# Two heads of a chunked mixer: where row broadcasts, staging transfers and transposing loads stand in their queues

## The chip, the cores and the metric

The kernel runs on one NeuronCore of one Trainium2 chip. The engines that matter here are TensorE (PE in the profile; its weight loads are PEld), VectorE (DVE), ScalarE (ACT), GpSimd (POOL) and SyncE (SP). SP issues the plain loads, POOL issues the transfers of this document's second part, and ACT issues the transposing loads. Each engine works through one queue in order: what stands behind a waiting instruction waits too. The metric is the device time of one launch in microseconds, lower is better. The median of three runs before is 1336.8 us, with 1336.1 us and 1338.56 us at the ends.

## What is computed

A two-layer backbone over 256 context tokens and 256 latent tokens of width 1024. Layer 0 mixes tokens with a bidirectional mLSTM of four heads, layer 1 with multi-head latent attention; a gated ConvFFN follows each. Only the mLSTM of layer 0 is touched. Cut to what matters, in each of its two directions:

```python
q, k = jnp.split(x_c @ w_qk, 2, axis=-1)               # 4 heads of 256
v = x_m @ w_v                                           # 4 heads of 512
dmat = where(tril, b[..., :, None] - b[..., None, :] + ic[..., None, :], -inf)
wmat = exp(dmat - mj[..., None]) * einsum("bhjd,bhsd->bhjs", q, k)
h = einsum("bhjs,bhse->bhje", wmat, v) / maximum(abs(sum(wmat, -1)), exp(-mj))[..., None]
out = head_rms_norm(sigmoid(h_in @ w_og) * (h_forward + h_backward)) @ w_out
```

The reference runs it in chunks of 64 with a carried state. The kernel computes the same sums over all 512 tokens at once: one 512-wide row of scores for each of four tiles of 128 tokens, weighted by exponentials of gate sums, in both directions.

## The kernel before

All matrix products are made of float32 numbers cut into a high and a low part (`split`, L460: an ACT cast makes the high part, a DVE subtraction the low one). Each product is three matmuls (`mm3`, L444): high by high, high by low, low by high. So each weight tile of 512 KB is loaded by SP, cast on ACT (L361) and subtracted on DVE (L384) before PE can use it; three such tiles `w` exist at a time.

**The loop over heads** (`build`, L2442 to L2458) interleaves two heads. While PE makes the queries and keys of head h (`w_qk`, L1024: four tiles j of 128 columns, two for the queries and two for the keys, each in two sections of 24 matmuls, so eight sections in all), DVE and ACT work on head h - 1 in small steps. After every section `tick(2, ...)` takes two steps of that background work, so a head has 16 steps. Behind the eight sections come the product of head h - 1's weights with its values (`av`, L1232) and the scores of head h (`s_mm`, L1042).

**What a background step is.** For head h - 1 the generator `head` (L1066) broadcasts two rows of gate sums over 128 partitions (tiles aB0 and aB1, DMAs on POOL's queue, L1070), adds a mask to them (Am0, Am1, DVE, L1075), makes the weights W of the four token tiles in three groups (ACT exponentials L1112, DVE products and normalisation L1113 to L1130), and transposes them on PE into PT (L1147). It ends with `t4_step(2)`, which issues two transfers from the packed weights into the DRAM tiles `t4d` (L1781). In these heads they are plain copies of 512 KB or 256 KB, the first terms of sums that later steps of the same list accumulate. Each is pinned behind the POOL instruction that was traced just ahead of it.

For head h - 2 the generator `post` (L1249) normalises the head's output and, in its second step, rearranges each of the four token tiles into two 16-bit planes (ACT, L466) and stores them in DRAM (tile hd, POOL's queue, L1265). Later, `turn_load` (L1298) reads them back transposed, one quarter at a time (tile hx, a transposing DMA on ACT's queue, L1306), and `turn_split` (L1309) cuts each quarter into the high and low parts hn (L1314 and L1315), which the output product `mout` reads after the loop.

**`mixed`** (L1285) has the order of both generators written out as 16 words, one for each step: h is a step of `head`, p one of `post`, L a `turn_load`, S a `turn_split`, a dot nothing. It runs in the stages of w_qk(2), with head 1 and the post step of head 0, and of w_qk(3), with head 2 and the post step of head 1. These two stages are what the change touches. Ahead of section 6 (tile j = 3, first half) `w_qk` calls `v_load` (L1197), which loads four value tiles vr and four gate tiles oh over POOL's queue and cuts the values.

**What sets the order.** The program is traced in this order and then ordered by a scheduler: each engine's queue takes instructions by their place in the trace, but one whose inputs and tile slot are at hand may go earlier. `behind` (L453) adds an order without a wait between two instructions of one engine. The tiles aB, Am, W, S, pl, hx, vr, oh and some others share one pool of 15 slots (tag `s2`).

Of the kernel before, what the change touches and what calls it, by code (L numbers as in the profile page):

```python
# [10 lines left out]
U16 = mybir.dt.uint16  # L11
# [405 lines left out]
class K:  # L417
# [40 lines left out]
                    mybir.DependencyClass.NoSync, mybir.DependencyReason.DATA), reason="behind")  # L458

    def split(self, hi, lo, src):  # L460
        self.nc.scalar.copy(hi, src)
        self.nc.vector.tensor_sub(lo, src, hi)

    def planes(self, dst, src):

        i = self.nc.scalar.copy(dst, src.bitcast(U16).rearrange("p (n h) -> p h n", h=2))  # L466
        return i
# [556 lines left out]
    def w_qk(self, h, nt, early=None):  # L1024
        self.qk = getattr(self, "qk", {})
        for j in range(4):
            m = (h * 2 + j) if j < 2 else (8 + h * 2 + j - 2)
            ps = self.ps("qk")
            for c in range(2):
                if early is not None and (j, c) == VE[h]:  # L1030
                    early()
                w = self.st.use(("qk", m, c))
                for kk in range(8):
                    k = 8 * c + kk
                    cs = slice(kk * 128, (kk + 1) * 128)
                    self.mm3(ps, (w[0][:, cs], w[1][:, cs]), (self.xc[k][:, 0], self.xc[k][:, 1]), k == 0, k == 15)
                self.tick(nt, ADA_Q)
            u = self.u("qk")
            self.split(u[:, 0], u[:, 1], ps)
            self.qk[h, j] = u  # L1040

    def s_mm(self, h):  # L1042
# [23 lines left out]
    def head(self, h, S, big=False):  # L1066
        nc, last = self.nc, big
# [2 lines left out]
            nc.gpsimd.dma_start(aB[d], self.ad[d, h:h + 1, :].to_broadcast([128, 512]))  # L1070
        if h == 0:
            self.t4_step(2)
        Am = [self.s2("Am0"), self.s2("Am1")]
        for d in range(2):
            nc.vector.tensor_tensor(Am[d].rearrange("p (t s) -> p t s", t=4),  # L1075
# [5 lines left out]
        for g in range(3):  # L1081
# [9 lines left out]
            for i, t in enumerate(jbs):  # L1091
                base = 256 * i if g == 0 else 0
                for d in range(2):
# [3 lines left out]
                    if d == 0:  # L1097
                        if t > 0:
                            spans.append((0, t * 128, aB[d]))
                        lo, hi = 0, (t + 1) * 128  # L1100
                    else:
# [6 lines left out]
                        lo, hi = {0: (0, 256), 1: (128, 256), 2: (0, 512), 3: (0, 512)}[t]  # L1108
# [11 lines left out]
            e = self.gcol[:, 1, jbs[0]:jbs[-1] + 1, h::32]  # L1120
# [3 lines left out]
            for i, t in enumerate(jbs):  # L1124
                big = {0: 1, 1: 0, 2: 1, 3: 0}[t]
# [15 lines left out]
        for grp in ([(t, s) for s in range(2) for t in (0, 1)], [(t, s) for s in range(2) for t in (2, 3)],  # L1141
# [3 lines left out]
            for n, (t, s) in sorted(enumerate(grp), key=lambda x: -x[1][0] * (x[1][0] > 1)):  # L1145
                src, b0 = P[t]
                q = nc.tensor.transpose(pt[:, n * 128:(n + 1) * 128], src[:, b0 + s * 128:b0 + (s + 1) * 128], self.ident)  # L1147
# [4 lines left out]
            u = self.u("PT")  # L1152
            self.split(u[:, 0], u[:, 1], pt)
            for n, x in enumerate(grp):
                self.PT[x] = u, slice(n * 128, (n + 1) * 128)
        if not last:
            self.t4_step(2)
        yield

    def head_turn(self, P):  # L1160
# [36 lines left out]
    def v_load(self, h):  # L1197
        nc = self.nc
        self.vh, self.oh = [], []
        for s in range(4):  # L1200
            r = self.s2("vr")
            nc.gpsimd.dma_start(r, self.vd[h, s])
            u = self.u("v")
            self.split(u[:, 0], u[:, 1], r)
            self.vh.append(u)
        for s in range(4):
            o = self.s2("oh")
            nc.gpsimd.dma_start(o, self.od[h, s])
            self.oh.append(o)

    def v_steps(self, h):

        nc = self.nc
        self.vh, self.oh = [], []
        for s in range(4):
            if s % 2 == 0:
                r = self.uf("vr")
            c = slice((s % 2) * 512, (s % 2 + 1) * 512)
            nc.gpsimd.dma_start(r[:, c], self.vd[h, s])
            u = self.u("v")  # L1220
            self.split(u[:, 0], u[:, 1], r[:, c])
            self.vh.append(u)
            yield
        for s in range(4):
            if s % 2 == 0:
                o = self.uf("oh")
            c = slice((s % 2) * 512, (s % 2 + 1) * 512)
            nc.gpsimd.dma_start(o[:, c], self.od[h, s])
            self.oh.append(o[:, c])
            yield  # L1230
# [53 lines left out]

    def mixed(self, head, post):  # L1285

        plan = "p hp h hL h hL . L S hLS h S S . . ."
        for step in plan.split():
            for op in step:
                if op in "hp":  # L1290
                    next(head if op == "h" else post, None)
                elif op == "L":
                    self.turn_load()
                elif op == "S":
                    self.turn_split()
            yield

    def turn_load(self):  # L1298

        h, d, e = self.turned[0]  # L1300
        if e == 3:
            self.turned.pop(0)
        else:
            self.turned[0] = h, d, e + 1
        x = self.s2("hx")
        self.nc.scalar.dma_start_transpose(x.bitcast(U16), d.rearrange("t h n -> (t h) n")[:, e * 128:(e + 1) * 128])  # L1306
        self.hx.append((h * 4 + e, x))

    def turn_split(self):  # L1309
# [134 lines left out]
    def aout_fin(self, o1, pl, xr, gate, fi, h1u, att):  # L1444
# [86 lines left out]
        def cols(t, pts, n):  # L1531
            mod(t, 0, pts)
            for k in range(0, n, 2):
                mod(t, k + 1, pts)
                split(t, k, 0)
                split(t, k + 1, 0)
                if k + 2 < n:
                    mod(t, k + 2, pts)
                split(t, k, 1)
                split(t, k + 1, 1)  # L1540
# [1063 lines left out]
```

## Time and profile before

| what | time |
|---|---|
| runs: median, lowest, highest | 1336.8, 1336.1, 1338.56 us |
| the profiled execution | 1337.46 us |
| its span, first to last instruction | 1335.3 us |
| outside the span | 2.16 us |
| DVE busy, share of the span | 1074.8 us, 80% |
| ACT busy, share of the span | 731.1 us, 55% |
| POOL busy, share of the span | 165.2 us, 12% |

The last four come from the page's first part. A group of instructions is named by its line in the kernel, its engine and its operation, with the tile written, an arrow and the tiles read. In the timeline the columns are start, duration (over all of a merged row), engine, line, operation, tiles, form and count, and in brackets the time that the engine sat idle before, with what ended it. An engine name with a q is the sequencer of that engine, which issues DMAs. In the view of one tile the last line gives the time from issue to landing of its DMAs. A matmul of 128x512 is shown with 0.39 us but the next starts about 0.23 us after it, since they are pipelined; starts, not durations, tell PE's pace.

### The profile page before, as it was taken

The page shows a single profiled execution, that of the slowest core. Times are in us where ns is not written, and L with a number is a line of the kernel's source. Part 1 is how long each engine was busy: PE and PEld are TensorE (multiplying, and loading weights), DVE is VectorE, ACT ScalarE, POOL GpSimd, SP SyncE. Part 2 cuts the span into 40 slices and gives each one's busy share as a digit, 9 for nine tenths or more (in the row PEclk, how much of TensorE's full clock was granted, in tenths as well). Part 3 has the DMA queues.
Part 4 walks back from the last instruction along what each step waited for, and adds up shares of the span by engine and source line. Part 5 has one row for each costly group of instructions (what it writes and reads, how often), then busy time and mean ns, then how long its engine had stood idle before and what let it go on. Part 6 is the DMA issues. An engine that isn't in the chain of part 4 may idle for free.

```text
span 1335.3 us, 18738 instructions
## 1 busy us (share of the span) xinstructions
PE 1324.6 (99%) x6561; PEld 1110.5 (83%) x6561; DVE 1074.8 (80%) x1784; ACT 731.1 (55%) x1275; POOL 165.2 (12%) x268
## 2 busy tenths in 40 slices
PE   9999999999999999999999999999999999999997
PEld 5877888888888888888898888888888988988886
DVE  4798957678687796987879977758899889899996
ACT  4765544446734655574644333333467768577771
POOL 0222000011101111120002011112000022120010
PEclk9999999999999999999999999999999999999999
DMA  9988948789678687885628989967876597499690
GB/s 368 332 279 281 337 164 257 233 271 306 242 239 240 179 244 199 298 277 209 223 80 272 324 263 283 278 170 187 310 245 212 179 243 205 154 317 298 228 333 36
DMA packets 122030, 327.10 MB, mean 245 GB/s; under 512 B 24792, under 2 KB 45528, under 8 KB 121664
## 3 DMA queue, kind: packets, MB, share of 16 engines
q1 hardware_dynamic: 64432, 223.50, 49.0%
q0 software_dynamic: 33360, 81.43, 22.6%
q10 hardware_dynamic: 24144, 20.98, 5.3%
q8 instruction: 51, 0.84, 0.2%
q14 instruction: 43, 0.35, 0.1%
HBM read 289.51 MB, written 57.58 MB: 260 GB/s over the span
## 4 chain that ended last, share of the span: by engine, by line
PE 87%; issue 10%; DVE 1%; DMA 1%; POOL 1%; ACT 0%; ACTq 0%; DVEq 0%; POOLq 0%
PE fin L1612 8%; PE y L450 6%; PE y L447 6%; PE y L451 6%; PE tok L447 6%; PE tok L450 6%; PE tok L451 6%; PE fin L450 6%; PE fin L451 6%; PE fin L447 6%; PE up L743 2%; PE up L447 2%; PE up L450 1%; PE up L451 1%; PE y L1455 1%
## 5 line engine op out<-in xcount | busy, mean ns | idle before, releaser
L384 DVE TENSOR_TENSOR w<-raw,w 128x1024 fp32r<-128x1024 f32 (+2 forms) x280 | 335.1, 1200 | 113.7 <-ACT w L361 109.6
L361 ACT CAST w<-raw 128x1024 fp32r<-128x1024 f32 (+2 forms) x280 | 289.7, 1036 | 248.9 <-PE tok L451 74.4
L566 DVE SCALAR_TENSOR_TENSOR junk<-ar,bc 128x1024 f32<-128x1024 f32 x128 | 155.7, 1217 | 6.0 <-DMA raw<-in_ws 2.3
L450 PE MATMUL fin<-h,w 128*128 128x512 f32 (+1 forms) x370 | 139.6, 377 | 0.0
L447 PE MATMUL fin<-h,w 128*128 128x512 f32 (+1 forms) x370 | 139.5, 377 | 0.0
L451 PE MATMUL fin<-h,w 128*128 128x512 f32 (+1 forms) x370 | 139.3, 377 | 0.0
L1612 PE MATMUL fin<-h,w 128*128 128x512 f32 (+1 forms) x636 | 113.0, 337 | 0.0
L1612 PEld LDWEIGHTS fin<-h,w 128*128 128x128 f32 x636 | 98.4, 189 | 13.4
L451 PE MATMUL qk<-xc,w 128*128 128x512 f32 x256 | 99.7, 390 | 0.3 <-DVE w L384 0.3
L447 PE MATMUL qk<-xc,w 128*128 128x512 f32 x256 | 99.9, 390 | 0.0
L450 PE MATMUL qk<-xc,w 128*128 128x512 f32 x256 | 99.6, 389 | 0.0
L450 PEld LDWEIGHTS fin<-h,w 128*128 128x128 f32 x370 | 69.6, 188 | 13.0
L447 PEld LDWEIGHTS fin<-h,w 128*128 128x128 f32 x370 | 69.6, 188 | 12.8
L451 PEld LDWEIGHTS fin<-h,w 128*128 128x128 f32 x370 | 69.6, 188 | 12.6
L384 DVE TENSOR_TENSOR wu<-raw,wu 128x1024 fp32r<-128x1024 f32 (+1 forms) x52 | 61.9, 1205 | 3.1 <-ACT wu L361 2.8
L451 PEld LDWEIGHTS qk<-xc,w 128*128 128x128 f32 x256 | 48.0, 188 | 10.6 <-DVE w L384 0.7
L450 PEld LDWEIGHTS qk<-xc,w 128*128 128x128 f32 x256 | 48.1, 188 | 10.0
L447 PEld LDWEIGHTS qk<-xc,w 128*128 128x128 f32 x256 | 48.1, 188 | 9.9
L361 ACT CAST wu<-raw 128x1024 fp32r<-128x1024 f32 (+1 forms) x52 | 52.8, 1045 | 5.5 <-DMA raw<-in_ws 5.5
L760 ACT ACTIVATE fg<-fg 128x512 f32<-128x512 f32 (+1 forms) x44 | 23.1, 525 | 57.8 <-DVE fg L758 51.7
L447 PE MATMUL tok<-w,hT 128*128 128x512 f32 x128 | 49.9, 390 | 0.0
L450 PE MATMUL tok<-w,hT 128*128 128x512 f32 x128 | 49.8, 389 | 0.0
(523 smaller groups left out, 3154.6 us busy)
## 6 DMA issues: line engine op xcount, KB each, us to landing
raw<-in_ws SPq DMA_DIRECT2D x279, 512.0 KB, 5.4
ar<-in_adaT SPq DMA_DIRECT2D x80, 512.0 KB, 5.7
t4d<-in_ws POOLq DMA_DIRECT2D x20, 512.0 KB, 8.7
zd<-in_ws POOLq DMA_DIRECT2D x18, 512.0 KB, 8.8
adaw<-in_ada SPq DMA_DIRECT2D x16, 512.0 KB, 7.9
raw<-zd SPq DMA_DIRECT2D x12, 512.0 KB, 5.7
zr<-fd ACTq DMA_DIRECT2D x33, 128.0 KB, 5.4
xmd<-xr POOLq DMA_DIRECT2D x16, 256.0 KB, 4.7
```

Source lines behind the costliest of these rows:

```text
L361: self.cast = k.nc.scalar.copy(h[:, :cols], src)
L384: i = self.k.nc.vector.tensor_sub(l[:, :n], src, h[:, :n])
L447: q = mm(out, w[0], x[0], start=start, stop=False, skip_group_check=on)
L450: mm(out, w[0], x[1], start=False, stop=False, skip_group_check=on)
L451: mm(out, w[1], x[0], start=False, stop=stop, skip_group_check=on)
L566: nc.vector.scalar_tensor_tensor(o, w, 1.0, self.bc[j], op0=ALU.mult, op1=ALU.mult, accum_out=col[:, k, j:j + 1])
L743: nc.tensor.matmul(ps[m], wk[i][:, c], hT[k][:, j], start=made[m] == 0, stop=made[m] == 23)
L760: nc.scalar.activation(tmp[:, :n], tmp[:, :n], AF.Silu)
L1455: q = mm(ps, x[a][:, ts], w[b][:, cs], start=k == 0 and n == 0, stop=k == 7 and n == 2)
L1612: self.nc.tensor.matmul(ps[:, 0:256] if x else ps, w[x][:, k * 128:(k + 1) * 128], h[:, 0:256] if x else h, start=i == 0 and not k0, stop= ...
```

## The change

Five edits in the stages of w_qk(2) and w_qk(3):

- `head` gets one more step of its own for heads 1 and 2: the broadcasts of aB alone, then a yield, then the masks. The plan's first word becomes `hp` instead of `p`, so the broadcasts are traced ahead of the plane stores instead of behind them. The masks stay in the second step and the three groups of W in the third to fifth.
- The step that makes PT moves from the tenth word to the ninth. Both come after the same section of matmuls.
- The two `t4d` transfers are no longer traced at the end of `head` but at the end of `v_load`, behind the four vr and four oh loads (for heads 1 and 2; head 0 keeps its own).
- The four turning loads move from steps 4, 6, 8 and 10 to steps 13 and 14, and each is ordered on ACT's queue behind `qcast`, the cast of the latest finished tile of w_qk. At steps 13 and 14 that is tile j = 2.
- The four turning splits move from steps 9, 10, 12 and 13 to steps 15 and 16.

```diff
     def split(self, hi, lo, src):
-        self.nc.scalar.copy(hi, src)
+        i = self.nc.scalar.copy(hi, src)
         self.nc.vector.tensor_sub(lo, src, hi)
+        return i
@@ w_qk
             u = self.u("qk")
-            self.split(u[:, 0], u[:, 1], ps)
+            self.qcast = self.split(u[:, 0], u[:, 1], ps)
@@ head
         if h == 0:
             self.t4_step(2)
+        elif not big:
+            yield
...
-        if not last:
-            self.t4_step(2)
         yield
@@ v_load
             nc.gpsimd.dma_start(o, self.od[h, s])
             self.oh.append(o)
+        if h:
+            self.t4_step(2)
@@ mixed
-        plan = "p hp h hL h hL . L S hLS h S S . . ."
+        plan = "hp hp h h h h . . h h . . LL LL SS SS"
@@ turn_load
         x = self.s2("hx")
-        self.nc.scalar.dma_start_transpose(x.bitcast(U16), d.rearrange("t h n -> (t h) n")[:, e * 128:(e + 1) * 128])
+        q = self.nc.scalar.dma_start_transpose(x.bitcast(U16), d.rearrange("t h n -> (t h) n")[:, e * 128:(e + 1) * 128])
+        self.behind(q, [self.qcast])
         self.hx.append((h * 4 + e, x))
```

No arithmetic changes, and no instruction is added or taken away on any engine.

## The prediction

> **What bounds the kernel now.** The page first.
>
> ```profile
> span 1335.3 us, 18738 instructions
> PE 1324.6 (99%) x6561; PEld 1110.5 (83%) x6561; DVE 1074.8 (80%) x1784; ACT 731.1 (55%) x1275; POOL 165.2 (12%) x268
> PE 87%; issue 10%; DVE 1%; DMA 1%; POOL 1%; ACT 0%; ACTq 0%; DVEq 0%; POOLq 0%
> ```
>
> PE is busy for 99% of the span and carries the chain that ended last. A change that takes no matmul away can win only where PE stands still. The waits of PE name four such places in the whole kernel; two lie in w_qk:
>
> ```profile
> PE PT L1147 <- DVE W L1130: 0.5, 1, 0.5
> PE qk L451 <- DVE w L384: 0.3, 1, 0.3
> ```
>
> Where are they? The timeline of PE, at the first matmul of w_qk(2), of av(1), of w_qk(3) and of av(2):
>
> ```profile
> 456.12 0.39 PE L447 MATMUL qk<-xc,w 128*128 128x512 f32 x1
> 500.98 0.39 PE L447 MATMUL av<-v,PT 128*128 128x512 f32 x1
> 513.32 0.39 PE L447 MATMUL qk<-xc,w 128*128 128x512 f32 x1
> 559.39 0.39 PE L447 MATMUL av<-v,PT 128*128 128x512 f32 x1
> ```
>
> Both stages run the same 204 instructions on PE: 192 matmuls and 12 transposes. w_qk(2) takes 500.98 - 456.12 = 44.86 us, w_qk(3) takes 559.39 - 513.32 = 46.07 us. w_qk(2) is full; w_qk(3) loses 1.21 us. The timeline of PE shows where:
>
> ```profile
> 535.31 0.39 PE L450 MATMUL qk<-xc,w 128*128 128x512 f32 x1
> 535.96 0.50 PE L451 MATMUL qk<-xc,w 128*128 128x512 f32 x1 [0.26 <-DVE w L384]
> ...
> 541.08 0.60 PE L1147 MATMUL PT<-ident,W 128*128 128x128 f32 x4
> 542.13 1.07 PE L1147 MATMUL PT<-ident,W 128*128 128x128 f32 x8 [0.46 <-DVE W L1130]
> ```
>
> First, section 4 (of 0 to 7) waits for the low part of its weights: 0.65 us between two starts instead of 0.23. Then eight of the twelve transposes wait for the last weights of head 2. With the slower starts just behind each wait these make up the 1.21 us. DVE was late both times, so what made DVE late?
>
> ```profile
> 517.76 0.55 POOL L1265 DMA_DIRECT2D hd<-pl  x1 [31.20 <-ACT pl L466]
> ...
> 519.25 0.54 POOL L1070 DMA_DIRECT2D aB<-ad  x1
> 521.53 0.54 POOL L1070 DMA_DIRECT2D aB<-ad  x1 [0.38 <-issue]
> 522.06 1.04 POOL L1781 DMA_DIRECT2D t4d<-in_ws  x2
> ...
> 523.34 0.69 DVE L1075 TENSOR_TENSOR Am<-aB,mask 128x512 f32<-128x512 f32 x1 [5.85 <-DMA aB<-ad]
> 528.25 0.69 DVE L1075 TENSOR_TENSOR Am<-aB,mask 128x512 f32<-128x512 f32 x1 [1.94 <-DMA aB<-ad]
> 528.98 0.40 ACT L1112 ACTIVATE W<-Am,gcol 128x128 f32<-128x128 f32 x1 [4.51 <-DVE Am L1075]
> 529.15 1.18 ACTq L1306 DMA_TRANSPOSE hx<-hd  x1
> 532.61 1.05 ACT L361 CAST w<-raw 128x1024 fp32r<-128x1024 f32 x1
> 534.68 1.22 DVE L384 TENSOR_TENSOR w<-raw,w 128x1024 fp32r<-128x1024 f32 x1
> ```
>
> Those rows are from the timelines of POOL, DVE and ACT, engine by engine but in order of time. The second broadcast leaves at 521.53, behind the plane stores, and its mask runs at 528.25 after idle time. ACT stands idle 4.51 us for that mask, then runs the exponentials of W back to back; the cast of section 4's weights is queued behind them, and DVE subtracts at 534.68, ready only at 535.90. PE wanted it near 535.5. The chain is: late broadcast, late mask, blocked ACT, late weights.
>
> **The change, part by part.**
>
> *Broadcasts ahead of the stores.* Nothing is added; the two issues change places with four stores. POOL was idle 31.20 us before 517.76, so both broadcasts can be out by 517.76 + 0.54 = 518.3: 3.2 us earlier for the second, or more if slots are free earlier. The view of the tile aB gives the landings, of the one issued at 519.25 and of the one issued at 521.53:
>
> ```profile
> DMA to landing us min/median/max: 4.1/4.1/4.1
> DMA to landing us min/median/max: 6.6/6.6/6.6
> ```
>
> The second mask so comes between 518.3 + 4.1 = 522.4 and 518.3 + 6.6 = 524.9, against 528.25: 3.3 to 5.8 us earlier. I take the 4.1 us, since that broadcast had the fewer stores ahead. Section 4's weights were late by about 0.4 us and the transposes' W by about 0.6 us; even 3.3 us covers both. Worth 1.21 us in w_qk(3) and nothing in w_qk(2), which has no loss. The stores leave two issues, 1.1 us, later; their readers move by some 20 us, so that costs nothing. The mask stays in the step where it was, so the extra yield costs nothing; if the order made it later after all, the 3.3 to 5.8 us are the cover.
>
> *The t4d copies behind the head's loads.* Two issues of 0.52 us each. They go behind the last gate load, ahead of the output product, whose first matmul is the second row:
>
> ```profile
> 544.68 0.54 POOL L1208 DMA_DIRECT2D oh<-od  x1 [5.80 <-DVE hn L1315]
> 571.73 0.39 PE L447 MATMUL y<-w,hn 128*128 128x512 f32 x1
> ```
>
> The copies themselves land, by the view of the tile t4d in that stage, in
>
> ```profile
> DMA to landing us min/median/max: 7.4/7.4/7.5
> ```
>  They leave the stretch of the second broadcast and enter 539 to 553, beside the loads of the output product's weights, whose first matmul is at 571.73. The price lies between 0 and, if those loads came late by the whole 7.4 us, still 0, for there are 18 us in hand. On the gain side the copies can explain at most 6.6 - 4.1 = 2.5 us of the second broadcast's landing, and part one already takes it. I count 0. Behind them on POOL stand head 3's broadcasts, 0.5 us each copy later, needed only after 571.73.
>
> [...] The second broadcast landed in 6.6 us though its copies were issued after it. [...]
>
> *Turning loads behind the third tile.* Issue times on ACT's sequencer and landing, from the view of tile hx over both stages; then, from the timelines, the subtractions of the values in both stages and the cast of the third tile in the second:
>
> ```profile
> L1306 ACTq DMA_TRANSPOSE hx<-hd x8: 1174/1237/1439, 470.4 to 533.2; - x8
> DMA to landing us min/median/max: 3.7/3.9/4.3
> ...
> 495.39 2.48 DVE L462 TENSOR_TENSOR v<-vr,v 128x512 fp32r<-128x512 f32 x4
> 548.71 0.59 ACT L461 CAST qk<-qk 128x512 fp32r<-128x512 f32 x1 [1.29 <-PE qk L451]
> 554.04 2.49 DVE L462 TENSOR_TENSOR v<-vr,v 128x512 fp32r<-128x512 f32 x4
> ```
>
> Four issues hold the sequencer 4 x 1.237 = 4.9 us. They leave 529 to 534, where ACT runs back to back anyway (gain 0 to 4.9 us on ACT, taken as 0: the exponentials ran on between the issues), and come behind the cast at 548.71. Behind them then may stand the four value casts, a weight cast, and the cast of tile j = 3. I take the cost as 0, because the value casts are traced ahead of the loads; the other end is the first rival. The splits come last: loads out by 554, landed 4 us later, splits done near 562, while hn is read from 571.73 on. The eight splits of the two stages keep their total on both engines. Head 3's broadcasts wait for the slots of these splits already (POOL idle for them at 544.68 too) and gain the slots that hx held early.
>
> *Sum.* Against the profiled execution: 1337.46 us, of which 2.16 us lie outside the span; 1335.3 - 1.2 = 1334.1 us span, 1336.3 us in all. That execution is 0.66 us above the median of 1336.8 us; against the median the forecast is 1336.8 - 1.2 = **1335.6 us**.
>
> **The rivals.**
>
> *The turning loads stand ahead of the value casts* (slower). Then the casts start 4.9 us later. Slack before: the values of head 1 are done at 495.39 + 2.48 = 497.87, 3.1 us ahead of av(1) at 500.98; of head 2 at 556.53, 2.9 us ahead of av(2). PE would wait 1.8 and 2.0 us, and the cast of tile j = 3 behind them may add some. 1336.8 - 1.2 + 3.8 = 1339.4 us. It decides once three of the four loads (3.7 us) precede the casts. For it: ACT takes its queue in order and the loads need nothing but the tile cast. Against: the values are traced first, and their loads left long before that cast, by the timeline of POOL:
>
> ```profile
> 534.22 2.20 POOL L1202 DMA_DIRECT2D vr<-vd  x4 [11.12 <-issue]
> ```
>
> *The waits stay* (no change). The broadcasts move, but DVE is as full as before: by the windows view (window, its length, then busy PE, PEld, DVE, ACT and POOL) 9.87 us of 540 to 550 and all of 550 to 560. If the order places other work, say the ada products, into the time won, weights and W come as late as now: 1336.8 us. Against: DVE idled 5.85 and 1.94 us for the broadcasts, so there is time to fill.
>
> ```profile
> 540.00:550.00 10.00, 9.54 (x49) 7.89 (x48) 9.87 (x17) 5.09 (x10) 0.54 (x1) 1.00 0.94 346
> 550.00:560.00 10.00, 10.00 (x46) 8.29 (x45) 10.00 (x15) 4.41 (x7) 1.08 (x2) 1.00 0.68 226
> ```
>
> *Half.* One wait goes, the transposes still wait, since W's last product is ordered behind DVE work of others: 1336.8 - 0.6 = 1336.2 us.
>
> **How the numbers follow.** A measurement of this kernel tells about 0.2%, 2.7 us, from no change. Forecast 56%, no change 20%, half 14%, loads ahead of the casts 10%. No case gives 2.7 us of gain: the two stages lose 1.21 us in all. I leave 3% for a better order elsewhere. Of the slower rival, which ends at 2.6 us with an open end, I put 7% over the bound. So faster 0.03, same 0.90, slower 0.07. The range takes the forecast with the scatter of the runs (0.7 us below the median to 1.8 us above), no change and half: 1334.3 to 1338.2 us.
>
> **What would show it.** Right: both aB issues ahead of hd on POOL; the second mask before 525; no idle ACT ahead of the first exponentials; no PE wait in w_qk(3), which then takes 44.9 us; loads of hx after 548; copies after the last oh. Wrong: a PE wait at the first matmul of av or of the scores; the value casts behind DMA_TRANSPOSE on ACT; a new PE wait in the output product for weights. The forecast falls if the stage after w_qk(3) starts to wait by more than 1.2 us.

## The result and the profile after

The changed kernel takes 1352.04 us (median of 5 runs, 1344.72 to 1354.74) beside 1337.19 us of the kernel before (1336.1 to 1338.56). The ratio is 1.0102, with a 95% interval of 1.0083 to 1.0121. The forecast was 1335.6 us with a range up to 1338.2: wrong in sign and outside the range.

The profiled execution is the quickest of the five, 1344.72 us, so it shows the loss at its smallest. From its page, the lines that answer to those of before (span, busy time of each engine, and the chain that ended last):

```profile
span 1342.9 us, 18743 instructions
PE 1328.1 (99%) x6561; PEld 1112.3 (83%) x6561; DVE 1074.3 (80%) x1784; ACT 731.3 (54%) x1275; POOL 165.1 (12%) x268
PE 55%; DVE 3%; issue 1%; ACTq 1%; ACT 1%; DMA 0%; DVEq 0%
```

Each engine counts as many instructions as before (the five more of the first line belong to the sequencers, which these counts leave out). But the chain, which held PE for 87% of the span, now follows PE for 55% only and passes through ACTq, the sequencer that issues the turning loads. (Its shares no longer add up to a whole, so they are not read further.) The waits of PE name what is new:

```profile
PE sc L447 <- ACT qk L461: 2.2, 2, 1.9
PE PT L1150 <- DVE W L1133: 1.7, 2, 0.9
```

The score matmuls now wait for the cast of the last tile of w_qk, j = 3, and the transposes into PT for W. Where the time goes is read from the first matmuls on PE's timeline: of w_qk(2), av(1), w_qk(3), av(2) and the output product y.

```profile
457.23 0.39 PE L447 MATMUL qk<-xc,w 128*128 128x512 f32 x1
...
502.10 0.39 PE L447 MATMUL av<-v,PT 128*128 128x512 f32 x1
...
515.58 0.39 PE L447 MATMUL qk<-xc,w 128*128 128x512 f32 x1
...
561.52 0.39 PE L447 MATMUL av<-v,PT 128*128 128x512 f32 x1
...
578.45 0.39 PE L447 MATMUL y<-w,hn 128*128 128x512 f32 x1
```

Against the starts of before (456.12, 500.98, 513.32, 559.39, 571.73) the stages compare like this. "av and scores" is from the first matmul of av to the first of the next stage.

| stage | before | after | lost |
|---|---|---|---|
| w_qk(2) | 44.86 | 44.87 | 0.01 |
| av(1) and scores | 12.34 | 13.48 | 1.14 |
| w_qk(3) | 46.07 | 45.94 | -0.13 |
| av(2) and scores | 12.34 | 16.93 | 4.59 |

The span is 7.6 us longer. Of these, 5.6 us lie in the four rows, 1.1 us ahead of w_qk(2) (457.23 against 456.12, a figure that moves by as much between kernels that do the same work there), and the rest in the output product behind. Nothing was gained in w_qk(3), where all the gain was expected.

The timeline of ACT and its sequencer in w_qk(3) shows the cause of the largest row:

```profile
550.84 0.59 ACT L461 CAST qk<-qk 128x512 fp32r<-128x512 f32 x1 [3.79 <-PE qk L451]
551.01 1.38 ACTq L1309 DMA_TRANSPOSE hx<-hd  x1
551.32 1.66 ACT L461 CAST v<-vr 128x512 fp32r<-128x512 f32 x3
552.42 5.52 ACTq L1309 DMA_TRANSPOSE hx<-hd  x1
552.88 0.62 ACT L461 CAST v<-vr 128x512 fp32r<-128x512 f32 x1
...
557.98 9.35 ACTq L1309 DMA_TRANSPOSE hx<-hd  x2
567.43 1.05 ACT L361 CAST w<-raw 128x1024 fp32r<-128x1024 f32 x1 [12.98 <-PE av L451]
568.39 1.33 ACT L1318 ACTIVATE hn<-hx,sm 128x512 fp32r<-128x512 f32 x2
...
571.47 0.57 ACT L461 CAST qk<-qk 128x512 fp32r<-128x512 f32 x1
```

The value casts (v) ran by 553.5, so they were not late. But the four issues, 1.2 us each before, took 1.38 and 5.52 us and, in one row, 9.35 us for the last two. ACT stood still for 12.98 us behind them. Then came four splits of the turned planes, and only at 571.47 the cast of tile j = 3, whose last matmul had started at 561.29: ACT took its queue in order. The timeline names "PE av" as what ended the 12.98 us, but the last issue ends at 557.98 + 9.35 = 567.33 and the cast starts at 567.43. The view of the tile hx over this stage gives the landings. It knows them for two of the four loads, and in other stages and runs too for a part of the loads only:

```profile
L1309 ACTq DMA_TRANSPOSE hx<-hd x4: 1375/4656/5522, 551.0 to 562.8; - x4
...
DMA to landing us min/median/max: 8.1/10.0/11.9
```

In the same stage before, the two that are known took 3.7 and 4.0 us; now it is 8.1 and 11.9 us. In w_qk(2), where the loads moved by as much, the issues took 1.2 to 2.6 us and the one known landing 4.0 us. What PE makes of w_qk(3):

```profile
569.91 0.28 PE L451 MATMUL sc<-qk 128*128 128x256 f32 x1
572.09 0.39 PE L447 MATMUL sc<-qk 128*128 128x256 f32 x1 [1.90 <-ACT qk L461]
573.05 0.39 PE L450 MATMUL sc<-qk 128*128 128x256 f32 x1 [0.58 <-DVE qk L462]
...
574.42 0.63 PE L450 MATMUL sl<-qk 128*128 128x512 f32 x1
574.84 0.63 PE L451 MATMUL sl<-qk 128*128 128x512 f32 x1
```

The waits come to 2.5 us, yet the stage loses 4.6: after them matmuls of 128x512 start 0.43 us apart instead of 0.23, up to 577.4. The windows view of this stretch (window, length, busy PE, PEld, DVE, ACT, POOL, then granted clock, share of the DMA engines, GB/s) has the clock at 0.78 of full speed, an average over the window; from 574.3 to 577.6 it is 0.50:

```profile
572.00:576.00 4.00, 3.34 (x14) 2.74 (x15) 4.00 (x6) 2.97 (x4) 0.00 (x0) 0.78 0.35 119
```

So the question for the experiments is why the four transposing loads of w_qk(3), moved by some 20 us, hold ACT for 16 us in place of 5.

### The profile page after: what moved, and what is told of

Its sections match the earlier page's. It is cut to its first block, busy times and chain, and to the rows that moved or that the text cites. A ratio compares the mean times of both kernels' runs of the same rounds, so it can differ in the third digit from the quotient of the medians.

```text
span 1342.9 us, 18743 instructions
## 1 busy us (share of the span) xinstructions
PE 1328.1 (99%) x6561; PEld 1112.3 (83%) x6561; DVE 1074.3 (80%) x1784; ACT 731.3 (54%) x1275; POOL 165.1 (12%) x268
## 2 busy tenths in 40 slices
DMA packets 122030, 327.10 MB, mean 244 GB/s; under 512 B 24792, under 2 KB 45528, under 8 KB 121664
## 4 chain that ended last, share of the span: by engine, by line
PE 55%; DVE 3%; issue 1%; ACTq 1%; ACT 1%; DMA 0%; DVEq 0%
PE fin L1616 8%; PE fin L450 6%; PE fin L451 6%; PE fin L447 6%; PE y L450 6%; PE y L451 6%; PE y L447 6%; PE y L1459 1%; ACTq L1309 1%; PE fin L1552 1%; PE s L2344 1%; PE PT L2365 1%; PE zT L1407 1%; DVE W L1116 0%; PE dkv L447 0%
```

## The experiments

Three theories stood at the beginning. **A**: in the new place the transposing packets share the DMA engines with ordinary loads, both lose speed, the issues hold ACT, and what stands behind them comes late. **B**: only the order on ACT hurts, the loads and splits standing ahead of the cast of tile j = 3. **C**: the broadcasts of the next head, which moved as well, are what the turning loads collide with.

### The change once more

No edit; four runs and a second profile.

> The changed kernel as it is, a second time. All theories: 1345 to 1355 us again. What its trace is to show: in the first profile PE waits 2.2 us for the cast of tile j = 3 ahead of the scores and then runs nine matmuls at 0.427 us instead of 0.23. If the slower executions differ by the length of that wait, this trace shows waits of several us ahead of the scores of both heads, each followed by slow matmuls; if they differ elsewhere, the two stages look as in the first profile.

Measured: 1350.65 us (1349.18 to 1355.02) beside 1337.24, ratio 1.0107 (1.0086 to 1.0128). From the waits of PE in its profile:

```profile
PE sc L447 <- ACT qk L461: 6.4, 2, 5.5
```

The same place, with a longest wait of 5.5 us in place of 1.9; av(2) and the scores take 21.40 us, 9.1 more than before. The expected wait of several us ahead of the scores of both heads came at head 3 alone, at head 2 it is 0.9 us. The size varies from run to run, the place does not.

### Part 3 alone

The broadcasts and the t4d copies stay where they were; only the turning loads and splits move:

```diff
-        plan = "p hp h hL h hL . L S hLS h S S . . ."
+        plan = "p hp h h h h . . h h . . LL LL SS SS"
...
+        self.behind(q, [self.qcast])
```

> The third part alone: turning loads behind the third tile and splits last; broadcasts and copies stay as before. Theory A (the transposing loads collide with whatever DMA traffic is there, hold ACT's queue, and the cast of tile j = 3 behind them is late): 1343 to 1355 us, waits ahead of the scores in both heads. Theory C (it is the next head's broadcasts, freed by the first part, that collide with them): w_qk(2) has no such broadcasts now, its transposing loads land in about 4 us, no wait ahead of the scores of head 2, and the total is 1337 to 1345 us.

Measured: 1354.35 us (1348.88 to 1362.7), ratio 1.0129 (1.0085 to 1.0173). All of the loss is in part 3. PE's longest wait ahead of the scores is 10.7 us in this profile; w_qk(3) takes 50.86 us too, with a wait of 1.9 us for a weight cast. From the waits of PE, and the tile hx over both stages:

```profile
PE sc L447 <- ACT qk L461: 10.7, 1, 10.7
```

```profile
L1307 ACTq DMA_TRANSPOSE hx<-hd x8: 1176/2079/11366, 491.8 to 575.8; - x8
...
DMA to landing us min/median/max: 7.8/10.1/18.2
```

And the last row of POOL's timeline ahead of the turning loads of w_qk(2), which leave from 491.8 on:

```profile
475.81 2.12 POOL L1209 DMA_DIRECT2D oh<-od  x4 [2.21 <-DVE W L1114]
```

POOL issued nothing from 478 to 522, so no broadcast was in flight in this stage. Still its second turning load held ACT's sequencer for 2.98 us, and the one whose landing is known took 10.1 us, so the loads of SP's queue, issued at 489.69, 492.63 and from 494.11 on, were enough to slow the turning loads. But PE did not wait ahead of the scores of head 2, as theory C expected and theory A did not; its 10.7 us are in w_qk(3), where two broadcasts left at 559.18 and 560.11, between an issue of 8.2 us that began at 556.17 and one of 11.4 us at 564.43. This run alone does not clear the broadcasts of a share in that. The run with part 1 alone, below, does more: there issues of 5.5 and 5.7 us, at 469.40 and 526.60, stand far from any broadcast (the nearest leave at 438.08, 492.41, 494.93 and 549.12). So theory C falls as the sole cause; what the broadcasts add in w_qk(3) was not measured.

### Parts 1 and 2 without part 3

The changed kernel with the turning loads and splits at their old steps and without `behind`.

> The first two parts without the third: broadcasts ahead of the stores, copies behind the head's loads, turning loads and splits where they were. Theories A, B and C: the loss is gone, 1334.5 to 1337.5 us. The step of my prediction for the first part (both PE waits of w_qk(3) vanish) gives 1335.6 us; if early broadcasts let other work take DVE, the wait ahead of PT stays and it is 1336 to 1337 us. A loss of over 2 us here would acquit the turning loads.

Measured: 1336.54 us (10 runs; eight of 1335.92 to 1337.39, and 1342.42 and 1346.14), ratio 1.0003 (0.9986 to 1.002). In the profile w_qk(3) takes 44.89 us and both waits in it are gone. But w_qk(2) takes 45.36 us and av(1) with its scores 13.28 us, 0.5 and 0.9 us more than before, and turning loads land there in up to 13.0 us: the span, 1335.6 us, is no shorter than before. The two high runs have no profile.

### The splits behind the cast

The changed kernel, with the four splits of a head's turned planes ordered behind the split of tile j = 3, on ACT and on DVE:

```diff
-        plan = "hp hp h h h h . . h h . . LL LL SS SS"
+        plan = "hp hp h h h h . . h h . . LL LL . . SSSS"
...
-        nc.scalar.activation(u[:, 0], x, AF.Copy, scale=g[:, k:k + 1])
+        i = nc.scalar.activation(u[:, 0], x, AF.Copy, scale=g[:, k:k + 1])
...
+        self.behind(i, [self.qcast])
+        self.behind(j, [self.qlow])
```

> The changed kernel with the four turning splits ordered behind the cast and the subtraction of tile j = 3 on ACT and DVE. Theory B (only the place of the splits ahead of that cast costs): no wait ahead of the scores, 1335 to 1337 us. Theory A: the wait shrinks but ACT's queue is still held by the issues of the transposing loads, until just before the scores in w_qk(3): 1336 to 1345 us, with issues of 2 to 6 us instead of 1.2 in the trace.

Measured: 1347.94 us, ratio 1.0078 (1.0044 to 1.0112). The six runs fall into two groups, three of 1341.42 to 1343.55 us and three of 1352.33 to 1355.02, with the median between them; the profile is of the lower group. The waits ahead of the scores are gone, and the four stages of the table above are full. The waits of PE and the tile hx show a new one, behind them, in the output product:

```profile
PE PT L1151 <- DVE W L1134: 4.7, 2, 3.9
```

```profile
L1310 ACTq DMA_TRANSPOSE hx<-hd x8: 1176/1544/3795, 491.7 to 555.4; - x8
...
DMA to landing us min/median/max: 3.9/12.1/13.8
```

Theory B alone falls, and half of the runs lie above the range of theory A too. The issues are still held, the landings are slow as before, and now the weights W of head 3 are late. The order only decides who pays.

### Ordinary loads in the place of the turning loads

```diff
-        q = self.nc.scalar.dma_start_transpose(x.bitcast(U16), d.rearrange("t h n -> (t h) n")[:, e * 128:(e + 1) * 128])
+        q = self.nc.scalar.dma_start(x, self.od[h, e])
```

> The changed kernel, with each of the eight turning loads replaced by an ordinary load of the same bytes (128x512 f32) on the same queue, tied behind the same cast. It leaves out the transposition: the output product of the spatial heads takes gate rows in the place of the head's normalised output. Theory A (the transposing packets and the ordinary ones slow each other when they share the DMA engines, and ACT stands behind their issue): issues as short as an ordinary load's, no issue above 2 us, landings of 4 to 8 us, no PE wait above 1 us between 490 and 600, time 1334.5 to 1338. Rival D (the place is what hurts: four more loads of 256 KB in a stretch already full of loads, or the tie to the third tile's cast, whatever their kind): the casts of the tiles j = 3 stay late, PE waits 2 us or more ahead of the scores, time 1344 to 1353.

Measured: 1336.54 us (1335.82 to 1337.58, 10 runs), ratio 0.9993 (0.9983 to 1.0002). Queue, place, tie, bytes and the splits behind are those of the changed kernel, and the whole loss is gone. (The loads read the gate rows, so they do not depend on the plane stores either; in the changed kernel those leave by 527.6, long before the turning loads of this stage.) The tile hx over w_qk(3), then a window of this kernel in which these loads are in flight, and two of the changed one:

```profile
L1309 ACTq DMA_DIRECT2D hx<-od x4: 327/442/446, 548.6 to 549.9; - x4
...
DMA to landing us min/median/max: 5.1/5.2/5.3
```

```profile
552.00:556.00 4.00, 4.00 (x20) 3.30 (x19) 2.35 (x3) 2.18 (x4) 0.43 (x1) 1.00 1.07 315
```

```profile
556.00:560.00 4.00, 4.00 (x20) 3.30 (x19) 1.69 (x2) 0.00 (x0) 0.75 (x2) 1.00 1.08 200
560.00:564.00 4.00, 4.00 (x19) 3.31 (x18) 0.00 (x0) 0.00 (x0) 0.00 (x0) 1.00 1.43 135
```

The last two columns are the share of the DMA engines and GB/s. The share adds up the times of packets, so it can pass 1. With ordinary loads a share of 1.07 moves 315 GB/s. With transposing loads 1.08 and 1.43 move 200 and 135 GB/s, while ACT's busy time is 0.00 for 8 us. Rival D, that the place is simply too full, falls.

### The broadcasts alone

Part 1 by itself: the extra step of `head`, and the plan's first word `hp`; copies and turning loads as before.

> Part 1 alone: the row broadcasts ahead of the plane stores; copies and turning loads as before. The prediction's step: both PE waits in w_qk(3) go, that stage takes 44.9 us, time lower by 1.2 us at most, 1335 to 1337.5 beside a kernel before of 1336.8 to 1337.5. Theory A: the same as long as the turning loads meet no ordinary loads; where they now leave earlier than 529 and meet the t4d copies, hx lands in more than 6 us in place of 3.9, and the time may scatter upward by some us in some runs. Rival C (the moved broadcasts harm by themselves): slower than before by 3 us or more in every run.

Measured: 1336.95 us (10 runs, seven of 1335.65 to 1337.03, and 1340.81, 1343.14, 1351.59), ratio 1.0011 (0.9987 to 1.0034). Both waits in w_qk(3) are gone; it takes 44.88 us. But the weights of the head now start earlier, the turning loads go out from 464.4 on, beside a weight load of SP at 465.60 and value loads of POOL from 469.76 on, and collide in the old place too. The tile hx over both stages:

```profile
L1308 ACTq DMA_TRANSPOSE hx<-hd x8: 1177/1214/5706, 464.4 to 532.4; - x8
...
DMA to landing us min/median/max: 7.9/13.4/25.1
```

This is theory A again, with a cover: 25.1 us to land, and in the profiled run PE waits for nothing in these stages. The likely reason is that the loads leave at 522.0 to 532.4 in the second stage, where the changed kernel has 551.0 to 562.8, with that much more time ahead of the output product. The three high runs are unexplained; no profile of them exists.

### The copies alone

Part 2 by itself: the `t4d` copies behind the gate loads; broadcasts and turning loads as before.

> Part 2 alone: the t4d copies behind the last gate load of the head; broadcasts and turning loads as before. The prediction's step: 0 us, the two PE waits of w_qk(3) stay, time 1336.5 to 1337.8. If the copies and not the stores held the second broadcast up: it lands in about 4.1 us in place of 6.6, its mask runs near 525.8, one or both waits go, and the time is up to 1.2 us lower. Theory A: hx as before (issue 1.2 us, landing 3.9 us), so no PE wait above 1 us.

Measured: 1337.39 us (10 runs, 1336.22 to 1343.23), ratio 1.0007 (0.9996 to 1.0018). In w_qk(3), up to the second broadcast, POOL issues exactly what it issued before, in the same order, to within 0.1 us; only the two copies behind it are gone, and SP's next weight load leaves at 525.04 in place of 525.20. From the timelines of POOL and DVE, and the view of the tile aB from 515 to 522:

```profile
521.49 0.54 POOL L1070 DMA_DIRECT2D aB<-ad  x1 [0.39 <-issue]
```

```profile
526.18 0.69 DVE L1075 TENSOR_TENSOR Am<-aB,mask 128x512 f32<-128x512 f32 x1
```

```profile
DMA to landing us min/median/max: 3.9/4.3/4.6
```

The second broadcast lands in 4.6 us in place of 6.6, its mask runs at 526.18 in place of 528.25, and both waits of PE in the stage are gone. The first matmuls of w_qk(3) and of av(2) start at 514.47 and 559.35: 44.88 us in place of 46.07. In w_qk(2), where PE did not wait, the second broadcast lands in 4.9 us in place of 7.1. So the copies, issued *behind* the broadcast in the same queue, were what held it up. The median does not show the gain of that stage: the interval ends at 0.9996, and 1.2 us would be 0.9991.

### The turning loads on SP's queue

The changed kernel, with the turning loads issued by SP in program order, so that ACT is not held and their issues stand in one queue with those of the weight loads:

```diff
-        q = self.nc.scalar.dma_start_transpose(x.bitcast(U16), d.rearrange("t h n -> (t h) n")[:, e * 128:(e + 1) * 128])
-        self.behind(q, [self.qcast])
+        q = self.nc.sync.dma_start_transpose(x.bitcast(U16), d.rearrange("t h n -> (t h) n")[:, e * 128:(e + 1) * 128])
+        self.tc.keep_in_program_order(q)
```

> The changed kernel, with the turning loads issued from SP's queue, in the order in which the program has them, behind the weight loads issued before them, and so no longer from ACT. Theory A in its strict form (engines that serve transposing and ordinary packets in turn lose throughput, and it is ACT's being held by the issue that reaches PE): one queue takes them one after the other, ACT is not held, PE waits ahead of the scores go, time 1335 to 1339; POOL's gate and broadcast loads still share engines with them, so that weight loads queued behind a turning load may land late, and then PE waits for weights instead. Theory B (the splits and casts queued ahead of tile j = 3 on ACT are enough): the waits ahead of the scores stay at 2 us or more, time 1344 to 1353.

Measured: 1342.53 us (1338.68 to 1346.16), ratio 1.0036 (1.0022 to 1.0049): between the two expectations. The two known landings in w_qk(3) fall to 5.9 and 8.0 us, but the loads go out late, from 556.84, behind six weight loads issued from 544.65 on, to 565.1, and ACT's timeline shows the splits waiting for them, with the cast of tile j = 3 behind:

```profile
564.85 0.72 ACT L1318 ACTIVATE hn<-hx,sm 128x512 fp32r<-128x512 f32 x1 [4.32 <-DMA hx<-hd]
...
569.51 0.72 ACT L1318 ACTIVATE hn<-hx,sm 128x512 fp32r<-128x512 f32 x1 [1.24 <-DMA hx<-hd]
570.13 0.57 ACT L461 CAST qk<-qk 128x512 fp32r<-128x512 f32 x1
```

PE waits 2.9 us for that cast. Theory A in its strict form, that the held issue is the only way to PE, falls; what was right in B is a second way.

### Both repairs together

SP's queue and the splits behind the cast.

> The changed kernel with both repairs at once: the turning loads leave from SP's queue, so that ACT is not held at their issue, and the splits of a head's turned planes are ordered behind the split of tile j = 3, so that this tile's cast does not stand behind them. Theory A, in the form left by the runs before (PE is reached on two ways, ACT held at the issue and the splits ahead of the cast; slow landings by themselves are covered, since the planes are read some 18 us later): no PE wait above 1 us anywhere between 440 and 620, hx may still land in 5 to 9 us, stages of 44.9, 12.3, 44.9 and 12.3 us, time 1335.5 to 1338.5. Rival E (the slowed transfers cost by themselves, through weights behind them on SP's queue or through head 3's broadcasts): the waits move to w, wu or W in the output product, which takes 103 us or more in place of 102.05, time 1339 to 1345.

Measured: 1337.96 us (1337.7 to 1341.18, 10 runs), ratio 1.0005 (0.9995 to 1.0015). No loss that can be told. The four medians of these two edits:

| | splits ahead of the cast | splits behind it |
|---|---|---|
| turning loads on ACT's queue | 1352.04 (the change) | 1347.94 |
| turning loads on SP's queue | 1342.53 | 1337.96 |

By these medians each edit takes its share away, 9.5 and 10.0 us for the queue, 4.1 and 4.6 us for the order. Three of the four steps are clear of the noise; the 4.1 us are not, since the intervals of the ratios, 1.0083 to 1.0121 and 1.0044 to 1.0112, overlap. The profiled run is the slowest of the ten, 1341.18 us, and has a wait of 2.5 us for W of head 3 in the output product, where theory A expected none above 1 us; to that extent rival E is right in single runs.

### Small packets without the transposition

Is it the transposing, or that a transposing load is made of small packets? The ordinary loads again, each read in 1024 pieces of 256 bytes:

```diff
-        q = self.nc.scalar.dma_start(x, self.od[h, e])
+        q = self.nc.scalar.dma_start(x.rearrange("p (c k) -> p c k", c=8), self.od[h, e].rearrange("p n -> (p n)").rearrange("(c p k) -> p c k", c=8, p=128, k=64))
```

> As the run with ordinary loads in the place of the turning loads, but each load of 256 KB is read in 1024 pieces of 256 bytes, in a permuted order, where that run read rows of 2 KB. It leaves out the transposition: the output product of the spatial heads takes permuted gate rows in the place of the head's normalised output. Theory A1 (it is the many small packets that slow the ordinary loads beside them): landings of hx of 8 us and more, issues above 2 us, PE waits of 2 us or more ahead of the scores or in the output product, time 1342 to 1353. Theory A2 (it is the transposing itself): landings of 4 to 7 us, no issue above 2 us, no PE wait above 1 us between 490 and 600, time 1335 to 1338, as with the ordinary loads.

The pages count the packets; of the changed kernel, of the ordinary loads, and of the small pieces:

```profile
DMA packets 122030, 327.10 MB, mean 244 GB/s; under 512 B 24792, under 2 KB 45528, under 8 KB 121664
```

```profile
DMA packets 114734, 327.10 MB, mean 245 GB/s; under 512 B 16472, under 2 KB 37208, under 8 KB 114368
```

```profile
DMA packets 121903, 327.10 MB, mean 244 GB/s; under 512 B 24665, under 2 KB 45401, under 8 KB 121537
```

Eight transposing loads are 24792 - 16472 = 8320 packets under 512 bytes, 1040 each; the pieces are 8193. Measured: 1340.74 us (1338.63 to 1342.58), ratio 1.0026 (1.0014 to 1.0037), against 1336.54 with large packets and 1352.04 with transposing ones. PE waits 2.3 us for W in the output product. The tile hx of the small pieces:

```profile
L1309 ACTq DMA_DIRECT2D hx<-od x8: 366/614/3502, 490.5 to 551.2; - x8
...
DMA to landing us min/median/max: 3.3/7.6/11.9
```

Neither expectation holds whole: theory A1 has the issues and the wait right, but its time too high. Packets of 256 bytes alone bring issues of up to 3.5 us and landings of up to 11.9 us, and cost about 4 us (1340.74 - 1336.54). The rest of the loss, some 11 us, comes with the transposing itself. How a DMA engine passes the two kinds is not shown by any run.

## Why the prediction was wrong

**What bounds the kernel** held: PE, and 1.21 us lost in w_qk(3). In every kernel where the turning loads were out of the way that stage is full: 44.89 us (parts 1 and 2), 44.88 (ordinary loads), 44.88 (part 1), 44.88 (part 2).

**Part 1** was right: both aB issues stand ahead of the stores (already in the stage before, at 494.83 and 495.43), the second mask followed the first at once at 523.56, and alone it removes both waits. In the changed kernel the gain does not show, since DVE, after waiting 3.55 us for a turned plane in the stage before, came to the masks late: 523.56 - 515.58 = 8.0 us into the stage, where with ordinary loads they ran 2.1 us into it (516.37 - 514.26). W was late again, and the stage takes 45.94 us.

**Part 2** had the right sum, but not the right shares. The prediction counted 0 because "part one already takes it". The measurement says otherwise: this part alone is worth 1.2 us in w_qk(3) (46.07 - 44.88), and the landing fell by 2.0 us with nothing moved but the copies behind. Either part is enough for that stage; together they bring no more there, and in the profile of both w_qk(2) and av(1) lose 1.4 us.

**Part 3** is the step that failed: "I take the cost as 0, because the value casts are traced ahead of the loads". The reason held as far as the value casts go, no run shows PE waiting for the values. The price did not: "Four issues hold the sequencer 4 x 1.237 = 4.9 us" used the issue time measured in the old place, where no weight load was issued beside them. In the new place in w_qk(3) the four issues took 1.38 + 5.52 + 9.35 = 16.2 us, and the two known landings 8.1 and 11.9 us in place of 3.9. Of the three things that "may stand" behind them (value casts, a weight cast, the cast of tile j = 3), the last two ran only behind the issues. "Splits done near 562" became 571.6. The prediction priced the moved loads by their row, but never asked what is in flight at the place they move to: SP's timeline of before shows it, six weight loads of 512 KB one upon the other in the very stretch that the turning loads move to, where the stretch they left had none issued from 525.6 to 535.9:

```profile
553.97 9.32 SPq L324 DMA_DIRECT2D raw<-in_ws  x6
```

By the sum with the measured sizes: cast of tile j = 3 at 571.47 in place of about 560, PE needs it at 570.0, 2.5 us of waits, and the other 2.1 us of the 4.6 behind them, at the slower clock for the most part.

**The clock** was left out of every rival. A PE wait of 2 us was priced at its own length. In five profiles with a PE wait of 1.9 us or more ahead of the scores or in the output product, the stretch lost 1.8 to 3.4 us beyond its waits: 4.6 us for 2.5 in the changed kernel, 9.1 for 5.9 in its second profile, 13.6 for 11.0 with part 3 alone, 6.7 for 3.4 with the turning loads on SP's queue, and 4.1 for 2.3 with the small pieces. Behind a wait of 0.88 us in w_qk(3) of the changed kernel the first two matmuls of 128x512 started 0.32 us apart, the next again 0.23. In the changed kernel, above, starts 572.09 - 569.91 = 2.2 and 573.05 - 572.09 = 1.0 us apart were followed by matmuls 0.43 us apart and a granted clock of 0.50 from 574.3 to 577.6. In the run with small pieces, below, it was one pause of 590.51 - 587.87 = 2.6 us with eight transposes behind it, and then starts 0.43 us apart from 591.91 to 594.89. How long a pause it takes, and whether the transposes count as idle, no run shows.

```profile
587.87 0.39 PE L451 MATMUL y<-wu,hn 128*128 128x512 f32 x1
590.51 1.06 PE L1150 MATMUL PT<-ident,W 128*128 128x128 f32 x8 [2.25 <-DVE W L1133]
...
592.34 0.63 PE L447 MATMUL y<-wu,hn 128*128 128x512 f32 x1
592.76 0.63 PE L450 MATMUL y<-wu,hn 128*128 128x512 f32 x1
```

**The rivals.** "The turning loads stand ahead of the value casts" had the right sign, the right engine and a time of 1339.4, but the wrong victim. "It decides once three of the four loads precede the casts": it decided although they did not, through the tile cast that the rival mentions in half a sentence. "The waits stay" and "half" did not come about.

**Open.** Why some runs of part 1 alone, and of parts 1 and 2, take 5 to 15 us more was not seen in a profile; that hx lands in up to 25.1 us there makes the same collision likely, but it is not shown. The same holds for a run of part 2 alone, at 1343.23 us. Open, too, is why the 1.2 us that w_qk(3) gains do not show in the median of part 2 alone; for the other kernels the intervals are too wide to tell. No kernel was faster than the one before beyond the measurement: the best medians, 1336.54 us, stand at ratios of 1.0003 and 0.9993 whose intervals contain 1.

## What to carry to other kernels

A transfer's issue time and landing belong to its place as well as to its kind: here a turning load took 1.2 to 1.4 us to issue and 3.7 to 4.3 us to land in the old place, up to 5.5 us (and 9.35 us for two) and 11.9 us in the new one, where an ordinary load of the same bytes took 0.44 and 5.2 us, and one in pieces of 256 bytes up to 3.5 and 11.9 us. Before moving a DMA, list what every other queue has in flight at the new place, and treat transposing or small-packet loads as ones that need a quiet stretch. An engine that issues a DMA can be held by it, as ACT stood still for 12.98 us in the changed kernel, so put such loads on a queue whose engine has nothing urgent behind them, and put the work that waits for them behind the work that PE waits for; here each of the two alone left a loss (1342.53 and 1347.94 us) and both together left none that can be told (1337.96 us). And price a wait of a busy PE above its length: in five profiles waits of 1.9 us and more cost 1.8 to 3.4 us beyond it, and where the starts behind them were read they were 0.43 us apart in place of 0.23.

## What the runs showed of the hardware

- A transposing load of 256 KB on ACT's queue: issue 1.2 to 1.4 us and landing 3.7 to 4.3 us in the kernel before, with no weight load issued from 467.1 to 477.2 and from 525.6 to 535.9, while they left; issue up to 11.4 us (part 3 alone) and landing up to 25.1 us (part 1 alone) beside ordinary loads.
- An ordinary load of the same size in the crowded place: issue 0.44 us, landing 5.2 us; read in pieces of 256 bytes: issue up to 3.5 us, landing up to 11.9 us.
- With turning loads, weight loads and two broadcasts in flight, 135 GB/s were moved in a window in which the 16 DMA engines show 1.43 as their share (560 to 564 in the changed kernel).
- Two plain copies issued behind a broadcast in the same queue lengthened its landing from 4.6 to 6.6 us, and from 4.9 to 7.1 us in the stage before.
- One pause of 2.6 us on PE, with eight transposes behind it, was followed by matmuls of 128x512 that started 0.43 us apart in place of 0.23, from 591.91 to 594.89 (small pieces); pauses of 2.2 and 1.0 us with one matmul between them by a clock of 0.50 from 574.3 to 577.6 (changed kernel).
